# Key and value compression in one set of float32r products instead of two sets of fp32 products

## The chip, the cores and the metric

The kernel runs on 1 core of one Trainium2 chip. The metric is device microseconds of one execution; three runs of the kernel before gave a median of 1655.65 us (1655.62 to 1655.7).

## The reference, cut to what matters

One decoder layer for 512 tokens of width 2048. A wide input projection feeds a sparse attention (mixer A) and a gated MLP (mixer B). The part that is changed is the first step of the attention's compressed branch: for keys and for values, blocks of 32 tokens at a stride of 16 are flattened together with a position embedding and go through a small two-layer network.

```python
def compress(kv, pe, w1, w2):
    b, s, g, d = kv.shape
    ch = kv.reshape(b, s // CMP_STRIDE, CMP_STRIDE, g, d)
    nc = s // CMP_STRIDE - CMP_RATIO + 1
    blocks = jnp.concatenate([ch[:, r:nc + r] for r in range(CMP_RATIO)], axis=2)
    blocks = blocks + pe[None, None, :, None, :]
    hid = jax.nn.silu(jnp.einsum('bnlgd,lde->bnge', blocks, w1))
    return jnp.einsum('bnge,ef->bngf', hid, w2)

kc = compress(k_c, pe_k, w1_k, w2_k)
vc = compress(v_c, pe_v, w1_v, w2_v)
```

There are 4 groups of 64 channels, so a block is 32 x 64 = 2048 numbers, and w1 is 2048 x 64 for keys and again for values.

## The kernel before, in words

**The stream of projections.** All large products are jobs of one generator, `gemm` (L170). A job is one block of columns of a weight matrix. Of kind "T" it holds 128 output columns, with the 512 tokens as the moving operand; each of its 16 steps over the 2048 inputs is one unit of three TensorE products (L190 to L192): the weights' high float32r part by the activations' high and low parts, and the weights' low part by the high part. Kind "N" has the tokens as the stationary operand (L198 to L200). A float32r part is a rounded copy (the high part) or what that rounding left (the low part). The weights are split while they stream in: SyncE's queue loads `raw`, ScalarE casts the high part (`high`, L98), VectorE subtracts for the low part (`low`, L104). `split_to` (L143) does this two sub-blocks of four steps ahead for the low part and three ahead for the high part. A job's evacuation `evac` empties its PSUM bank at the end; parts of it can be put off in `deferred`, which `flush` runs. `background` is a queue of small pieces of ScalarE and VectorE work, of which each sub-block takes two (`state["pops"]`).

**The order.** The program text fixes the order on each engine. `fill(n)` (L228) issues n more units of the stream, `finish(name)` (L232) issues units until that job is done. Everything that is not a projection is placed between such calls by hand. The jobs around the change are, in order, kc0, kc1 (compressed keys), vc0, vc1 (compressed values), k00, k01, k10, k11 (other keys), vs, vw (other values), q0, z0 and so on.

**The compression.** `evac_c` (L314) copies each of the four banks into `tokk` or `tokv`, fp32 tiles with two tokens folded onto the 128 partitions (64 channels each): two ScalarE copies (L320, L321) and two VectorE copies (L324, L325). Two further columns per tile hold the position embedding, put there after vc0 by a transpose (L680) and copies (L682, L683). After vc1, `hidden` (L687) runs once for keys and once for values: 16 fp32 products of 128 x 64 weights by 132 columns (4 groups of 32 blocks and one more), into one bank, with `fill(1)` after every fourth; then VectorE adds the embedding's part (L696, L698), ScalarE takes a tanh (L700), VectorE finishes SiLU (L701 to L708). The second layer is L717 (keys) and L722 (values), after which the stream goes on to q1. Between these stand `fill(4)`, `fill(6)` and `fill(6)`, so that with the eight inside `hidden` 24 units of k00 and k01 lie between the end of vc1 and L717.

**Other names the prediction uses.** `evac_k` (L249) empties the banks of k00 to k11 with four ScalarE casts (L254) and four VectorE subtractions (L256). `evac_v` (L260) empties those of vs and vw; L266 is a tanh on a part of vw's bank. `bank` (L68) hands out a whole PSUM bank, two to each of four tags. `o32` (L645) is a 16 KB per partition tile that the gates and the attention's outputs use later on.

Of the kernel before, what the change touches and what calls it, by code (L numbers as in the profile page):

```python
# [12 lines left out]
F32 = mybir.dt.float32  # L13
F32R = mybir.dt.float32r
BF16 = mybir.dt.bfloat16
AF = mybir.ActivationFunctionType
ALU = mybir.AluOpType
# [3 lines left out]
P = 128  # L21
# [3 lines left out]
KT = D // P  # L25
HEADS = 16
GROUPS = 4
HD = 64
NCMP = 32
EPS = 1e-6  # L30
MASKED = -3.0e32
C_Q, C_KV, C_G, C_ZA, C_UV, C_ZB, C_M = 0, 1024, 2560, 2608, 3632, 5680, 6704
# [19 lines left out]
def kernel(ctx: ExitStack, tc: tile.TileContext, x, p, norm_g, w_in,  # L52
                      pe_k, w1_k, w2_k, pe_v, w1_v, w2_v, ln_g, ln_b, sgu_w, sgu_b,
                      w_up_a, w_up_b, w_out, w_ple, w_ple_gate, final_g, out):
    nc = tc.nc
    x, out = x[0], out[0]
    p = p[0, 0]
    norm_g, w_in, ln_g, ln_b, sgu_w, sgu_b = norm_g[0], w_in[0], ln_g[0], ln_b[0], sgu_w[0], sgu_b[0]
    pe_k, w1_k, w2_k, pe_v, w1_v, w2_v = pe_k[0], w1_k[0], w2_k[0], pe_v[0], w1_v[0], w2_v[0]
# [8 lines left out]
    def bank(kind, name):  # L68
        return psum.tile([P, 512], F32, tag=kind, name=name)
# [26 lines left out]
    def high(hi, src, scale=None):  # L96
        if scale is None:
            nc.scalar.copy(hi, src)  # L98
        else:
            nc.scalar.mul(hi, src, scale)  # L100

    def low(hi, lo, src, scale=None):
        if scale is None:
            nc.vector.tensor_tensor(out=lo, in0=src, in1=hi.bitcast(F32), op=ALU.subtract)  # L104
        else:
            nc.vector.scalar_tensor_tensor(out=lo, in0=src, scalar=scale, in1=hi.bitcast(F32),
                                           op0=ALU.mult, op1=ALU.subtract)

    def split(hi, lo, src, scale=None, later=False):

        high(hi, src, scale)
        if later:
            deferred.append(lambda: low(hi, lo, src, scale))
        else:
            low(hi, lo, src, scale)
# [3 lines left out]
    background = deque()  # L119

    def add_job(job):
        first = 0
        while first < job.kt:
            n = min(job.per_load, job.kt - first)
            loads.append((job, first, n))
            for k in range(first, first + n, job.per_sub):
                subs.append((job, k, min(job.per_sub, first + n - k), len(loads) - 1))
            first += n
        jobs.append(job)
# [98 lines left out]
    def fill(n):  # L228
        for _ in range(n):
            next(run, None)  # L230

    def finish(name):  # L232
        while name not in done:
            next(run)
        flush()
# [76 lines left out]
    tok = {}  # L312

    def evac_c(which, a):  # L314
        def f(ps):
            t = tok[which]
            g0, g1 = 2 * a, 2 * a + 1
            src = ps.rearrange("p (n o e) -> p e o n", n=NCMP, o=8)
            lo_r, up_r = slice(0, 64), slice(64, 128)
            nc.scalar.copy(t[lo_r, :, g0, :NCMP], src[lo_r, 0])  # L320
            nc.scalar.copy(t[up_r, :, g0, :NCMP], src[lo_r, 1])  # L321

            def rest():
                nc.vector.tensor_copy(t[up_r, :, g1, :NCMP], src[up_r, 1])  # L324
                nc.vector.tensor_copy(t[lo_r, :, g1, :NCMP], src[up_r, 0])  # L325
            deferred.append(rest)
        return f

# [18 lines left out]
        add_job(Job(f"pl{cg}", "N", w_ple, 512 * cg, 512, 2, lambda k: (pl_in["h"][:, k], pl_in["l"][:, k]),  # L347
                    evac_ple(cg), (xs, ys)[cg % 2]))
    for a in range(2):
        add_job(Job(f"kc{a}", "T", w_in, C_KV + 128 * a, 128, KT, h_act, evac_c("k", a)))  # L350
    for a in range(2):
        add_job(Job(f"vc{a}", "T", w_in, C_KV + 256 + 128 * a, 128, KT, h_act, evac_c("v", a)))
    for b, c in ((0, 512), (1, 1024)):
        for a in range(2):
            add_job(Job(f"k{b}{a}", "T", w_in, C_KV + c + 128 * a, 128, KT, h_act, evac_k(b, a)))
# [190 lines left out]
    with tc.tile_pool(name="xin", bufs=4, side="right") as xin:  # L546
# [7 lines left out]
        st = xin.tile([P, TT, 2], F32, name="st", bufs=1)  # L554
# [35 lines left out]
        for j in range(2):  # L590
            b = bank("t", "ps_p")
# [4 lines left out]
        b = bank("o", "ps_g")  # L596
# [46 lines left out]
    vc = mid.tile([P, GROUPS, HD], F32, name="vc")  # L643
    orow = ph_o.enter_context(tc.tile_pool(name="orow", bufs=1, side="right"))
    o32 = orow.tile([P, 8, S], F32, name="o32")  # L645
# [14 lines left out]
                            base=-31, channel_multiplier=1)  # L660

    with tc.tile_pool(name="cmp", bufs=1) as cmp:
        w1t, w2t, pet = {}, {}, {}
        for n in "kv":
            tok[n] = cmp.tile([P, 8, GROUPS, NCMP + 2], F32, name="tok" + n)
            nc.gpsimd.memset(tok[n][:, :, :, NCMP:], 0.0)
        for n, w1, w2, pe in (("k", w1_k, w2_k, pe_k), ("v", w1_v, w2_v, pe_v)):
            w1t[n] = cmp.tile([P, 16, HD], F32, name="w1" + n)
            w2t[n] = cmp.tile([HD, 2, HD], F32, name="w2" + n)
            pet[n] = cmp.tile([NCMP, 2, HD], F32, name="pe" + n)  # L670
            for i in range(2):
                nc.gpsimd.dma_start(pet[n][:, i], pe)
        for n, w1, w2 in (("k", w1_k, w2_k), ("v", w1_v, w2_v)):
            nc.gpsimd.dma_start(w1t[n], w1.rearrange("l d e -> (l d) e").rearrange("(m p) e -> p m e", p=P))
            for i in range(2):
                nc.gpsimd.dma_start(w2t[n][:, i], w2)
        finish("vc0")
        for n in "kv":
            b = bank("t", "ps_pe")
            nc.tensor.transpose(b[:, :NCMP], pet[n].rearrange("l i d -> l (i d)"), ident[:NCMP, :NCMP])  # L680
            src = b[:, :NCMP].rearrange("p (s o e) -> p e o s", s=2, o=8)
            nc.vector.tensor_copy(tok[n][0:64, :, 0, NCMP:], src[0:64, 0])  # L682
            nc.vector.tensor_copy(tok[n][64:128, :, 0, NCMP:], src[64:128, 1])  # L683
        finish("vc1")
        hid = {}

        def hidden(n):  # L687
            b = bank("o", "ps_hid")
            o = b[:HD, :132].rearrange("p (g n) -> p g n", g=GROUPS)
            for m in range(16):  # L690
                nc.tensor.matmul(o, w1t[n][:, m], tok[n][:, m % 8, :, m // 8:m // 8 + NCMP + 1],
                                 start=m == 0, stop=m == 15)
                if m % 4 == 3:
                    fill(1)
            c = cmp.tile([HD, 1], F32, name="c" + n)
            nc.vector.tensor_copy(c, b[:HD, 32:33])  # L696
            y = cmp.tile([HD, GROUPS, NCMP], F32, name="y" + n)
            nc.vector.tensor_scalar(out=y, in0=o[:, :, :NCMP], scalar1=c, scalar2=None, op0=ALU.add)  # L698
            t = cmp.tile([HD, GROUPS, NCMP], F32, name="t" + n)
            nc.scalar.activation(t, y, AF.Tanh, scale=0.5)  # L700
            nc.vector.scalar_tensor_tensor(out=y, in0=t, scalar=1.0, in1=y, op0=ALU.add, op1=ALU.mult)  # L701
            if n == "k":
                h = cmp.tile([HD, GROUPS, NCMP], F32, name="hidk")
                nc.vector.tensor_scalar(out=h, in0=y, scalar1=0.5, scalar2=None, op0=ALU.mult)
            else:
                h = cmp.tile([HD, GROUPS, 4, NCMP], F32, name="hidv")
                for r in range(4):
                    nc.vector.tensor_scalar(out=h[:, :, r], in0=y, scalar1=0.5, scalar2=None, op0=ALU.mult)  # L708
            hid[n] = h

        fill(4)
        hidden("k")
        fill(6)
        hidden("v")
        fill(6)
        b = bank("o", "ps_kc")
        nc.tensor.matmul(b[:, :128], w2t["k"].rearrange("e i f -> e (i f)"),  # L717
                         hid["k"].rearrange("e g n -> e (g n)"), start=True, stop=True)
        split(kc_h, kc_l, b[:, :128].rearrange("p (g n) -> p g n", g=GROUPS))
        b = bank("o", "ps_vc")  # L720
        for g in range(GROUPS):
            nc.tensor.matmul(b[:, g * HD:g * HD + HD], hid["v"][:, g].rearrange("e r n -> e (r n)"),  # L722
                             w2t["v"][:, 0], start=True, stop=True)
        nc.vector.tensor_copy(vc, b[:, :256].rearrange("p (g d) -> p g d", g=GROUPS))
        finish("q1")

# [190 lines left out]
    n = len(slots)  # L917
# [40 lines left out]
    with tc.tile_pool(name="mlp", bufs=1) as mlp:  # L958
        vn = mlp.tile([P, TT, 1024], F32, name="vn")
        st = mlp.tile([P, TT, 2, 6], F32, name="bst")  # L960
# [10 lines left out]
        for hf in range(2):  # L971
            b = bank("o", "ps_w")
            for j in range(4):
                nc.tensor.transpose(b[:, j * P:j * P + P], ws[:, 4 * hf + j], ident)
            nc.vector.tensor_tensor(out=ws[:, 4 * hf:4 * hf + 4], in0=b.rearrange("p (g t) -> p g t", g=4),
                                    in1=tri.unsqueeze(1).to_broadcast([P, 4, P]), op=ALU.mult)
# [3 lines left out]
        with tc.tile_pool(name="uzp", bufs=1) as uzp:  # L980
# [36 lines left out]
            for g in range(8):  # L1017
# [3 lines left out]
                for gg in ((0, 1, 2) if g == 2 else (g,)):  # L1021
                    b = bank("st"[gg % 2], "ps_sv")
                    for c in range(TT):
                        nc.tensor.matmul(b[:, c * P:c * P + P], vn[:, c, gg * P:gg * P + P], ws[:, gg],
                                         start=True, stop=True)
                    sv = vn[:, :, gg * P:gg * P + P]
                    nc.vector.tensor_tensor(out=sv, in0=b.rearrange("p (c t) -> p c t", c=TT),
                                            in1=bs[:, gg].unsqueeze(1).to_broadcast([P, TT, P]), op=ALU.add)
                    nc.gpsimd.tensor_tensor(out=uz[:, gg].rearrange("p (c t) -> p c t", c=TT),
                                            in0=uz[:, gg].rearrange("p (c t) -> p c t", c=TT), in1=sv, op=ALU.mult)  # L1030
# [17 lines left out]
    for cg in range(4):  # L1048
# [50 lines left out]
```

## Time and profile before

| | |
|---|---|
| median of three runs | 1655.65 us |
| the profiled execution, its own time | 1655.33 us |
| its span, first to last instruction | 1653.6 us |
| TensorE (PE) busy in the span | 1639.1 us |
| VectorE (DVE) busy | 742.8 us |
| ScalarE (ACT) busy | 612.9 us |
| GpSimd (POOL) busy | 114.0 us |
| the two runs of `hidden`, first to last product's start | 84.1 to 102.7 us of the span |

How to read it: a row of the timeline gives the start in us from the span's start, the duration, the engine (PEld is TensorE's weight load), the line, the operation, the tile written and those read, the shapes and a count of merged instructions; in brackets stands the idle time of the engine ahead of it and what ended it. A matmul's shown duration is longer than the step from one start to the next, since they are pipelined, so costs are taken from the steps between starts. An fp32 product shows as two records (the 16 products of one `hidden` are x32). The times are of one execution; its own time is 1.7 us above its span.

### The profile page before, as it was taken

How to read it: one execution, taken by the hardware profiler on the slowest of the kernel's cores; microseconds unless marked ns; L12 is line 12 of the kernel's file. 1: busy time of each engine (PE TensorE's matmuls, PEld its weight loads, DVE VectorE, ACT ScalarE, POOL GpSimd, SP SyncE). 2: the span in 40 equal slices, each digit the busy share in tenths (PEclk: the TensorE clock that was granted, in tenths of full speed). 3: DMA queues.
4: the chain of work that ended last, by engine and by line, in shares of the span. 5: the costliest groups of instructions: out<-in, count | busy, mean ns of one | idle time of the engine just before them, and what ended most of it. 6: DMA issues, size and time to landing. Idle time of an engine off the chain costs nothing.

```text
span 1653.6 us, 20567 instructions
## 1 busy us (share of the span) xinstructions
PE 1639.1 (99%) x7837; PEld 1367.1 (83%) x7837; DVE 742.8 (45%) x1486; ACT 612.9 (37%) x1229; POOL 114.0 (7%) x145
## 2 busy tenths in 40 slices
PE   9999999999999999999999999999999999999997
PEld 7879988888888888888888888888888888888886
DVE  6443368888874363344222232223223433333335
ACT  7333356666663332233222222222223322223335
POOL 1200000110110001000000000000000000000001
PEclk9999999999999999999999999999999999999999
DMA  8522421111115333333333333333333533363333
GB/s 318 130 60 81 113 64 52 52 45 46 51 52 153 95 96 89 90 96 95 102 90 102 97 95 102 90 101 96 95 101 91 203 90 90 99 218 92 100 101 128
DMA packets 217186, 168.02 MB, mean 102 GB/s; under 512 B 4976, under 2 KB 190976, under 8 KB 215552
## 3 DMA queue, kind: packets, MB, share of 16 engines
q1 hardware_dynamic: 213472, 151.57, 32.7%
q0 software_dynamic: 3472, 14.79, 2.5%
q8 instruction: 61, 1.00, 0.2%
q14 instruction: 37, 0.30, 0.1%
q10 hardware_dynamic: 144, 0.36, 0.1%
HBM read 158.31 MB, written 8.39 MB: 101 GB/s over the span
## 4 chain that ended last, share of the span: by engine, by line
PE 97%; DVE 2%; ACT 1%; DMA 0%; issue 0%; DVEq 0%; SPq 0%; ACTq 0%
PE ps_wo L198 4%; PE ps_wo L200 4%; PE ps_mb L191 4%; PE ps_ma L191 4%; PE ps_ma L190 4%; PE ps_mb L192 4%; PE ps_mb L190 4%; PE ps_ma L192 4%; PE ps_wo L199 4%; PE ps_pg L198 3%; PE ps_pg L199 3%; PE ps_pg L200 3%; PE ps_t L805 2%; PE ps_za L190 2%; PE ps_za L192 2%; PE ps_za L191 2%
## 5 line engine op out<-in xcount | busy, mean ns | idle before, releaser
L104 DVE TENSOR_TENSOR lo<-raw,hi 128x512 fp32r<-128x512 f32 (+1 forms) x536 | 366.7, 687 | 641.0 <-PE ps_mb L192 129.5
L98 ACT CAST hi<-raw 128x512 fp32r<-128x512 f32 (+1 forms) x536 | 328.2, 615 | 724.1 <-PE ps_wo L200 99.2
L198 PE MATMUL ps_wo<-hi,act_h 128*128 128x512 f32 x256 | 101.0, 395 | 0.1
L200 PE MATMUL ps_wo<-hi,act_l 128*128 128x512 f32 x256 | 99.8, 390 | 0.0
L199 PE MATMUL ps_wo<-lo,act_h 128*128 128x512 f32 x256 | 99.7, 390 | 0.0
L190 PE MATMUL ps_ma<-act_h,hi 128*128 128x512 f32 x256 | 99.6, 389 | 0.0
L191 PE MATMUL ps_ma<-act_l,hi 128*128 128x512 f32 x256 | 99.6, 389 | 0.0
L192 PE MATMUL ps_ma<-act_h,lo 128*128 128x512 f32 x256 | 99.6, 389 | 0.0
L190 PE MATMUL ps_mb<-act_h,hi 128*128 128x512 f32 x256 | 99.6, 389 | 0.0
L191 PE MATMUL ps_mb<-act_l,hi 128*128 128x512 f32 x256 | 99.6, 389 | 0.0
L192 PE MATMUL ps_mb<-act_h,lo 128*128 128x512 f32 x256 | 99.6, 389 | 0.0
L98 ACT CAST pth<-ps_t 128x512 fp32r<-128x512 f32 (+1 forms) x88 | 48.0, 546 | 65.6 <-PE ps_t L805 65.3
L766 ACT ACTIVATE prob<-prob,st 128x512 f32<-128x512 f32 (+3 forms) x128 | 70.6, 555 | 3.9 <-DVE st L757 3.7
L444 POOL TENSOR_TENSOR m<-sig,sig 128x512 f32<-128x512 f32 x16 | 27.0, 1690 | 582.3 <-DVE sig L442 464.1
L104 DVE TENSOR_TENSOR ptl<-ps_t,pth 128x512 fp32r<-128x512 f32 (+1 forms) x88 | 56.2, 638 | 21.5 <-ACT pth L98 20.6
L757 DVE CUSTOM_DVE_ANT_0 prob<-ps_s,b 128x512 f32<-128x512 f32 (+3 forms) x128 | 56.3, 486 | 9.8 <-PE ps_s L754 9.4
L200 PEld LDWEIGHTS ps_wo<-hi,act_l 128*128 128x128 f32 x256 | 48.1, 188 | 10.3
L198 PEld LDWEIGHTS ps_wo<-hi,act_h 128*128 128x128 f32 x256 | 48.1, 188 | 10.1 <-DVE sig L442 0.5
L190 PEld LDWEIGHTS ps_mb<-act_h,hi 128*128 128x128 f32 x256 | 48.1, 188 | 10.0
L190 PEld LDWEIGHTS ps_ma<-act_h,hi 128*128 128x128 f32 x256 | 48.1, 188 | 10.0
L192 PEld LDWEIGHTS ps_ma<-act_h,lo 128*128 128x128 f32 x256 | 48.1, 188 | 10.0
L191 PEld LDWEIGHTS ps_mb<-act_l,hi 128*128 128x128 f32 x256 | 48.1, 188 | 9.9
(317 smaller groups left out, 3672.2 us busy)
## 6 DMA issues: line engine op xcount, KB each, us to landing
raw<-in_w_in_dram SPq DMA_DIRECT2D x164, 512.0 KB, 3.7
raw<-in_w_out_dram SPq DMA_DIRECT2D x32, 512.0 KB, 3.6
raw<-in_w_ple_gate_dram SPq DMA_DIRECT2D x32, 512.0 KB, 3.6
raw<-in_w_up_a_dram SPq DMA_DIRECT2D x16, 512.0 KB, 3.8
raw<-in_w_up_b_dram SPq DMA_DIRECT2D x16, 512.0 KB, 3.8
xt<-in_x_dram SPq DMA_DIRECT2D x4, 1024.0 KB, 11.5
spill<-ple POOLq DMA_DIRECT2D x4, 1024.0 KB, 6.8
m<-in_x_dram POOLq DMA_DIRECT2D x4, 1024.0 KB, 7.3
```

What stands on the lines that cost most here:

```text
L98: nc.scalar.copy(hi, src)
L104: nc.vector.tensor_tensor(out=lo, in0=src, in1=hi.bitcast(F32), op=ALU.subtract)
L190: nc.tensor.matmul(ps, hi[:, j], ah, start=st, stop=False)
L191: nc.tensor.matmul(ps, hi[:, j], al, start=False, stop=False)
L192: nc.tensor.matmul(ps, lo[:, j], ah, start=False, stop=sp)
L198: nc.tensor.matmul(o, ah[:, sl], hi[:, j], start=st, stop=False)
L199: nc.tensor.matmul(o, ah[:, sl], lo[:, j], start=False, stop=False)
L200: nc.tensor.matmul(o, al[:, sl], hi[:, j], start=False, stop=sp)
L444: nc.gpsimd.tensor_tensor(out=merge_tiles["m"][:, f], in0=merge_tiles[0], in1=t, op=ALU.add)
L757: nc.vector.tensor_tensor_reduce(out=pt[:, j * n:j * n + n], in0=o[:, j], in1=b0[:, 512 - n:], scale=-SLOPE[h], scalar=3.0e38, op0=ALU.add ...
L766: nc.scalar.activation(sl, sl, AF.Exp, bias=st[:, 0, j, hh:hh + 1], scale=-1.0, accum_out=st[:, 1, j, hh:hh + 1])
L805: nc.tensor.transpose(b[:, (2 * e + hh) * P:(2 * e + hh + 1) * P], pts[hh][:, c:c + P], ident)
```

## The change

Keys and values go through the first layer together, in float32r parts:

- The token tiles become `tokh` and `tokl`, a high and a low float32r part of 128 x 8 x 2 x 4 x 34, with keys and values side by side. `evac_c` now makes four ScalarE copies (high) and, put off in `deferred`, four VectorE subtractions (low) for each bank. The embedding's copies get a low part too.
- The two w1 matrices are loaded by the same GpSimd queue into `o32`, and are split into `w1h` and `w1l`, with keys' and values' 64 columns side by side, by four pieces of `background` that vc1's first two sub-blocks take up.
- The first layer is one loop of 16 steps with three products each: weights 128 x 128 by 272 columns (2 x 4 x 34). The first eight steps go to one bank, the last eight to another. Of the 128 x 272 results only keys by keys and values by values are used. ScalarE copies the first bank to `o32` after step 8; VectorE adds the shifted halves and the embedding's part, for the two halves of the partitions apart; then tanh and SiLU run once for both.
- Units of the stream around it: `fill(3)`, four inside the loop, `fill(8)`: 15 instead of 24 ahead of the second layer, which itself keeps its products.

```diff
     def evac_c(which, a):
         def f(ps):
-            t = tok[which]
-            g0, g1 = 2 * a, 2 * a + 1
+            th, tl = (tok[i][:, :, which] for i in "hl")
             src = ps.rearrange("p (n o e) -> p e o n", n=NCMP, o=8)
-            lo_r, up_r = slice(0, 64), slice(64, 128)
-            nc.scalar.copy(t[lo_r, :, g0, :NCMP], src[lo_r, 0])
-            nc.scalar.copy(t[up_r, :, g0, :NCMP], src[lo_r, 1])
+            halves = slice(0, 64), slice(64, 128)
+            part = [(halves[e], halves[r], 2 * a + r, e) for r in range(2) for e in range(2)]
+            for dst, srow, g, e in part:
+                nc.scalar.copy(th[dst, :, g, :NCMP], src[srow, e])
 
             def rest():
-                nc.vector.tensor_copy(t[up_r, :, g1, :NCMP], src[up_r, 1])
-                nc.vector.tensor_copy(t[lo_r, :, g1, :NCMP], src[up_r, 0])
+                for dst, srow, g, e in part:
+                    nc.vector.tensor_tensor(out=tl[dst, :, g, :NCMP], in0=src[srow, e],
+                                            in1=th[dst, :, g, :NCMP].bitcast(F32), op=ALU.subtract)
             deferred.append(rest)
...
+            for e, rows in enumerate((slice(0, 64), slice(64, 128))):
+                h, l = (tok[i][rows, :, n, 0, NCMP:] for i in "hl")
+                nc.vector.tensor_copy(h, src[rows, e])
+                nc.vector.tensor_tensor(out=l, in0=src[rows, e], in1=h.bitcast(F32), op=ALU.subtract)
+            for c in (slice(0, 8), slice(8, 16)):
+                background.append(lambda n=n, c=c: split(w1t["h"][:, c, n], w1t["l"][:, c, n], w1r[n][:, c]))
         finish("vc1")
...
+        while background:
+            fill(1)
+        fill(3)
+        hid = [bank("o", f"ps_hid{i}")[:, :8 * (NCMP + 2)] for i in range(2)]
+        for m in range(16):
+            o, st, sp = hid[m // 8], m % 8 == 0, m % 8 == 7
+            th, tl = (tok[i][:, m % 8].rearrange("p s g n -> p (s g n)") for i in "hl")
+            wh, wl = (w1t[i][:, m].rearrange("p s e -> p (s e)") for i in "hl")
+            nc.tensor.matmul(o, wh, th, start=st, stop=False)
+            nc.tensor.matmul(o, wh, tl, start=False, stop=False)
+            nc.tensor.matmul(o, wl, th, start=False, stop=sp)
+            if m == 7:
+                nc.scalar.copy(o32[:, 6, :8 * (NCMP + 2)], o)
+            if m % 4 == 3:
+                fill(1)
...
+        for n, rows in enumerate((lo_r, up_r)):
+            o, q = (t[rows].rearrange("p (s g n) -> p s g n", s=2, g=GROUPS)[:, n]
+                    for t in (o32[:, 6, :8 * (NCMP + 2)], hid[1]))
+            nc.vector.tensor_tensor(out=c[rows], in0=o[:, 0, NCMP:NCMP + 1], in1=q[:, 0, NCMP + 1:], op=ALU.add)
+            nc.vector.scalar_tensor_tensor(out=y[rows], in0=o[:, :, :NCMP], scalar=c[rows], in1=q[:, :, 1:NCMP + 1],
+                                           op0=ALU.add, op1=ALU.add)
+        nc.scalar.activation(t, y, AF.Tanh, scale=0.5)
+        nc.vector.scalar_tensor_tensor(out=y, in0=t, scalar=1.0, in1=y, op0=ALU.add, op1=ALU.mult)
+        for r in range(4):
+            nc.vector.tensor_scalar(out=h[:, :, r], in0=y, scalar1=0.5, scalar2=None, op0=ALU.mult)
+        fill(8)
```

More of the change, by code (lines that the diff above doesn't have):

```diff
@@ L349 @@
     for a in range(2):
-        add_job(Job(f"kc{a}", "T", w_in, C_KV + 128 * a, 128, KT, h_act, evac_c("k", a)))
+        add_job(Job(f"kc{a}", "T", w_in, C_KV + 128 * a, 128, KT, h_act, evac_c(0, a)))
     for a in range(2):
-        add_job(Job(f"vc{a}", "T", w_in, C_KV + 256 + 128 * a, 128, KT, h_act, evac_c("v", a)))
+        add_job(Job(f"vc{a}", "T", w_in, C_KV + 256 + 128 * a, 128, KT, h_act, evac_c(1, a)))
     for b, c in ((0, 512), (1, 1024)):
@@ L662 @@
     with tc.tile_pool(name="cmp", bufs=1) as cmp:
[L663 to L670, printed above, removed]
+        w1t, pet = {}, {}
+        for i in "hl":
+            tok[i] = cmp.tile([P, 8, 2, GROUPS, NCMP + 2], F32R, name="tok" + i)
+            nc.gpsimd.memset(tok[i].bitcast(F32)[:, :, :, :, NCMP:], 0.0)
+            w1t[i] = cmp.tile([P, 16, 2, HD], F32R, name="w1" + i)
+        w2t = o32[:, 4, 256:384].rearrange("p (i e) -> p i e", i=2)
+        for n, pe in enumerate((pe_k, pe_v)):
+            pet[n] = cmp.tile([NCMP, 2, HD], F32, name=f"pe{n}")
             for i in range(2):
                 nc.gpsimd.dma_start(pet[n][:, i], pe)
-        for n, w1, w2 in (("k", w1_k, w2_k), ("v", w1_v, w2_v)):
-            nc.gpsimd.dma_start(w1t[n], w1.rearrange("l d e -> (l d) e").rearrange("(m p) e -> p m e", p=P))
+        w1r = [o32[:, 2 * n:2 * n + 2].rearrange("p a (m e) -> p (a m) e", e=HD) for n in range(2)]
+        for n, w1 in enumerate((w1_k, w1_v)):
+            nc.gpsimd.dma_start(w1r[n], w1.rearrange("l d e -> (l d) e").rearrange("(m p) e -> p m e", p=P))
+        for n, w2 in enumerate((w2_k, w2_v)):
             for i in range(2):
-                nc.gpsimd.dma_start(w2t[n][:, i], w2)
+                nc.gpsimd.dma_start(w2t[64 * n:64 * n + 64, i], w2)
         finish("vc0")
-        for n in "kv":
+        for n in range(2):
             b = bank("t", "ps_pe")
@@ L681 @@
             src = b[:, :NCMP].rearrange("p (s o e) -> p e o s", s=2, o=8)
-            nc.vector.tensor_copy(tok[n][0:64, :, 0, NCMP:], src[0:64, 0])
-            nc.vector.tensor_copy(tok[n][64:128, :, 0, NCMP:], src[64:128, 1])
-        finish("vc1")
[L685 to L715, printed above, removed]
+            for e, rows in enumerate((slice(0, 64), slice(64, 128))):
[4 more added lines that the diff above has]
+                background.append(lambda n=n, c=c: split(w1t["h"][:, c, n], w1t["l"][:, c, n], w1r[n][:, c]))
@@ new lines @@
+        y = o32[:, 4, 0:128].rearrange("p (g n) -> p g n", g=GROUPS)
+        t = o32[:, 4, 128:256].rearrange("p (g n) -> p g n", g=GROUPS)
+        h = o32[:, 5].rearrange("p (g r n) -> p g r n", g=GROUPS, r=4)
+        c = cmp.tile([P, 1], F32, name="hid_c")
+        lo_r, up_r = slice(0, 64), slice(64, 128)
+        for n, rows in enumerate((lo_r, up_r)):
[4 more added lines that the diff above has]
+                                           op0=ALU.add, op1=ALU.add)
@@ L716 @@
+        nc.scalar.activation(t, y, AF.Tanh, scale=0.5)
[3 more added lines that the diff above has]
+        fill(8)
         b = bank("o", "ps_kc")
-        nc.tensor.matmul(b[:, :128], w2t["k"].rearrange("e i f -> e (i f)"),
-                         hid["k"].rearrange("e g n -> e (g n)"), start=True, stop=True)
+        nc.tensor.matmul(b[:, :128], w2t[lo_r].rearrange("e i f -> e (i f)"), h[lo_r, :, 0], start=True, stop=True)
@@ L721 @@
         for g in range(GROUPS):
-            nc.tensor.matmul(b[:, g * HD:g * HD + HD], hid["v"][:, g].rearrange("e r n -> e (r n)"),
-                             w2t["v"][:, 0], start=True, stop=True)
+            nc.tensor.matmul(b[:, g * HD:g * HD + HD], h[up_r, g].rearrange("e r n -> e (r n)"), w2t[up_r, 0],
+                             start=True, stop=True)
         nc.vector.tensor_copy(vc, b[:, :256].rearrange("p (g d) -> p g d", g=GROUPS))
```

## Prediction

> **What bounds the kernel now.** I read the profile's page first: busy times, slices, and the chain that ended last.
>
> ```profile
> PE 1639.1 (99%) x7837; PEld 1367.1 (83%) x7837; DVE 742.8 (45%) x1486; ACT 612.9 (37%) x1229; POOL 114.0 (7%) x145
> PEclk9999999999999999999999999999999999999999
> PE 97%; DVE 2%; ACT 1%; DMA 0%; issue 0%; DVEq 0%; SPq 0%; ACTq 0%
> ```
>
> TensorE is busy nearly throughout, at full granted clock, and makes 97% of the chain. So a microsecond taken off TensorE's queue comes off the end, and a wait put into it is added; work on the other engines counts only where TensorE waits for it. The change sits at 70 to 110 us of the span, so next comes TensorE's timeline there.
>
> ```profile
> 81.34 0.39 PE L190 MATMUL ps_k<-act_h,hi 128*128 128x512 f32 x1
> 83.83 0.39 PE L192 MATMUL ps_k<-act_h,lo 128*128 128x512 f32 x1
> 84.15 1.11 PE L691 MATMUL ps_hid<-tokk,w1k 128*64 128x132 f32 x8
> 85.19 0.50 PE L190 MATMUL ps_k<-act_h,hi 128*128 128x512 f32 x1
> 86.08 1.11 PE L691 MATMUL ps_hid<-tokk,w1k 128*64 128x132 f32 x8
> 89.97 1.11 PE L691 MATMUL ps_hid<-tokk,w1k 128*64 128x132 f32 x8
> ```
>
> From 81.34 to 83.83 are 11 steps of the stream: 2.49 / 11 = 0.227 us a product, 0.68 us a unit. From the first to the last of the four blocks of fp32 products are three periods, (89.97 - 84.15) / 3 = 1.94 us, each one block and one unit. **A block costs 1.94 - 0.68 = 1.26 us**, its turns into and out of fp32 included. The eight blocks cost 8 x 1.26 = 10.1 us.
>
> **The change part by part.** *The new products.* The trace has no float32r product of 272 columns, but it has them with 128 x 128 weights at 256 and 304.
>
> ```profile
> 149.97 0.28 PE L198 MATMUL ps_vs<-hi,act_h 128*128 128x256 f32 x1
> 153.93 0.28 PE L198 MATMUL ps_vs<-hi,act_h 128*128 128x256 f32 x1
> 160.77 0.30 PE L198 MATMUL ps_vw<-hi,act_h 128*128 128x304 f32 x1
> 167.39 0.30 PE L198 MATMUL ps_vw<-hi,act_h 128*128 128x304 f32 x1
> ```
>
> At 256 columns there are 33 products between the two rows, 3.96 / 33 = 0.120 us each; at 304 there are 48, 6.62 / 48 = 0.138 us. The price at 272 lies between; a third of the way gives 0.126. **16 x 3 = 48 products cost 6.05 us** (5.8 to 6.6). They follow float32r products, so I count no turn. This gains 10.1 - 6.05 = 4.05 us.
>
> *The first wait.* The second product of the new loop reads `tokl`, which is complete only when vc1's bank has been through four ScalarE copies and four VectorE subtractions. These rows show how it is emptied now:
>
> ```profile
> 81.54 0.37 ACT L320 COPY tokv<-ps_vc 64x256 f32<-64x256 f32 x1 [2.28 <-PE ps_vc L192]
> 81.92 0.36 ACT L321 COPY tokv<-ps_vc 64x256 f32<-64x256 f32 x1
> 82.31 0.43 DVE L324 COPY tokv<-ps_vc 64x256 f32<-64x256 f32 x1 [2.75 <-ACT tokv L321]
> 82.75 0.43 DVE L325 COPY tokv<-ps_vc 64x256 f32<-64x256 f32 x1
> 126.22 2.36 ACT L254 CAST ob_h<-ps_k 64x512 fp32r<-64x512 f32 x4 [2.29 <-PE ps_k L192]
> 128.61 2.80 DVE L256 TENSOR_TENSOR ob_l<-ps_k,ob_h 64x512 fp32r<-64x512 f32 x4 [4.37 <-ACT ob_h L254]
> 186.70 0.42 DVE L104 TENSOR_TENSOR vt<-ps_vw,vt 128x256 fp32r<-128x256 f32 x1 [0.32 <-ACT vt L98]
> 187.16 0.21 ACT L266 ACTIVATE gates<-ps_vw 128x48 f32<-128x48 f32 x1 [0.49 <-DVE vt L104]
> ```
>
> L324 needs nothing that L320 or L321 produce, and still starts 0.03 us after L321's end. In `evac_k` the first of four subtractions needs the first cast alone, and starts when all four have ended (126.22 + 2.36). L266 reads other columns than the subtraction it waits for. So two engines on one PSUM tile go one after the other, in program order. The four copies start at 81.54, 0.38 apart, and end at 81.54 + 3 x 0.38 + 0.37 = 83.05; the subtractions, taken at the 0.44 step and 0.43 duration of the 64x256 copies (a 64x512 one takes 2.80 / 4 = 0.70, half of it 0.35), run from 83.09 to 83.09 + 3 x 0.44 + 0.43 = 84.84. TensorE answers 0.05 us later, as at 132.19 below: 84.89. With `fill(3)` it gets there at 81.34 + 9 x 0.227 = 83.38 with the first product, which needs only `tokh`, and at 83.51 with the second. It stands for 84.89 - 83.51 = 1.38 us. Before, `fill(4)` and a ready tile by 83.18 hid this.
>
> *What a stand costs beyond itself, and a second wait.* The same kind of wait exists after evacuations by `evac_k`:
>
> ```profile
> 120.11 1.90 DVE L104 TENSOR_TENSOR lo<-raw,hi 128x512 fp32r<-128x512 f32 x3
> 120.12 0.39 PE L190 MATMUL ps_k<-act_h,hi 128*128 128x512 f32 x1
> 120.35 0.39 PE L191 MATMUL ps_k<-act_l,hi 128*128 128x512 f32 x1
> 120.86 0.50 PE L192 MATMUL ps_k<-act_h,lo 128*128 128x512 f32 x1
> 121.20 0.40 PE L190 MATMUL ps_k<-act_h,hi 128*128 128x512 f32 x1
> 123.98 0.39 PE L190 MATMUL ps_k<-act_h,hi 128*128 128x512 f32 x1
> 132.19 0.19 PEld L192 LDWEIGHTS ps_k<-act_h,lo 128*128 128x128 f32 x1 [0.54 <-DVE lo L104]
> ...
> PEld ps_k L192 <- DVE lo L104: 1.1, 2, 0.5
> ```
>
> VectorE comes late with `lo` because it was held by L256. From 120.12 to 123.98 are 15 steps, 15 x 0.227 = 3.40 in steady flow, 3.86 here: 0.46 us lost. The stand itself is 120.86 - 120.35 - 0.227 = 0.28; the restart takes the other 0.18. Hence the first wait costs **1.38 + 0.18 = 1.56 us**. The last row, from the list of waits (us in total, times, longest), counts it twice: after k01 and after k10. After k00 it is absent, since the values' fp32 blocks slowed TensorE there. In the new order L722 stands one unit ahead of k00's end (3 + 4 + 8 = 15 of 16), nothing slows k01, and VectorE and ScalarE meet the same queue: **0.46 us** for a third such wait, zero at the least.
>
> *VectorE's and ScalarE's added work.* In vc1 VectorE gets two more instructions for vc0's bank, four more small ones for the embedding, and four splits of 128x512, all queued around the stream's own.
>
> ```profile
> 70.19 0.37 ACT L320 COPY tokv<-ps_vc 64x256 f32<-64x256 f32 x1 [2.28 <-PE ps_vc L192]
> 71.85 0.17 DVE L682 COPY tokk<-ps_pe 64x16 f32<-64x16 f32 x1
> 72.03 0.18 DVE L683 COPY tokk<-ps_pe 64x16 f32<-64x16 f32 x1
> 72.61 1.51 DVE L104 TENSOR_TENSOR lo<-raw,hi 128x512 fp32r<-128x512 f32 x2
> 76.35 0.39 PE L192 MATMUL ps_vc<-act_h,lo 128*128 128x512 f32 x1
> ...
> L104 DVE TENSOR_TENSOR lo<-raw,hi 128x512 fp32r<-128x512 f32 (+1 forms) x536 | 366.7, 687 | 641.0 <-PE ps_mb L192 129.5
> ...
> 54.65 1.06 POOL L676 DMA_DIRECT2D w2v<-in_cmp_w_v_dram  x2
> DMA to landing us min/median/max: 7.6/7.6/7.6
> ```
>
> The first `lo`, now at 72.61, then follows copies to 71.70, four subtractions to 73.5 and eight small ones of 0.2, to 75.1; it ends at 75.8, and the product that needs it is the one at 76.35. The margin is 0.5 us, so I count nothing. Then two splits and a `lo` by turns, 0.69 each, end at 79.9, ahead of their products (79.1 for the next, done at 77.8; 81.8 for the one after). ScalarE's share, a cast ahead of each, ends sooner. The w1 loads keep GpSimd's queue, whose last issues of this group are over at 54.65 + 1.06; with w1v's 7.6 us to landing (last row) the data are there at 64, covered by 7 us and more. If any cover goes, the price is what it is late by.
>
> *Behind the loop.* ScalarE's copy of the first bank waits for step 8 in ScalarE's queue, ahead of casts not due for two sub-blocks. The loop ends at 84.89 + 46 x 0.126 + 4 x 0.68, about 93.5. VectorE's chain goes by these rows:
>
> ```profile
> 106.11 0.34 DVE L698 TENSOR_SCALAR yv<-ps_hid,cv 64x128 f32<-64x128 f32 x1
> 106.49 0.31 ACT L700 ACTIVATE tv<-yv 64x128 f32<-64x128 f32 x1 [3.63 <-DVE yv L698]
> 107.15 0.63 DVE L708 TENSOR_SCALAR hidv<-yv 64x128 f32<-64x128 f32 x4
> ```
>
> Four additions and a product at yv's 0.34, the tanh at 0.31, the halving at 0.63 and some gaps make about 3 us; `fill(8)` covers 8 x 0.68 = 5.4. It costs nothing. The second layer keeps its products and its price.
>
> **The sum:** 4.05 - 1.56 - 0.46 = 2.0 us gained. The span goes to 1651.6, the profiled execution to 1653.3, and the median, which stands 0.3 us above it, from 1655.65 to **1653.6 us**. That is 0.12%, inside the 0.2% (3.3 us) that a measurement of this kernel can tell from no change.
>
> **Rivals.** *A shorter first wait.* If a bank is shared by partitions, the first two subtractions, which read the lower 64 rows, start after the second copy at 82.31, and the third and fourth after the last, at 83.2: `tokl` is ready at 84.06, TensorE stands 0.6 us and loses 0.78, and the time is 1652.85. Taken to its end (only the last subtraction behind the last copy) it costs nothing: with no k00 wait either, the gain is 4.05, **1651.6**. Against it: L324 reads the upper rows while L320 and L321 read the lower, and waits. The Trainium skill, "PSUM — Partial Sum Buffer", section Terms, says that engines are kept apart per bank and 32-partition quadrant, and that different quadrants of a bank may be used at the same time. The trace does not agree that this kernel profits from it: L324's 0.03 us behind L321 is a whole-bank order.
>
> *No wait after k00.* Then 0.46 comes back: 1653.15. For it: the casts ahead may stand differently; against: k01 and k10 lose the same.
>
> *VectorE late in vc1.* If the small instructions or the w1 splits run longer than counted, the 0.5 us margin goes and one more restart comes on top: up to 1 us, 1654.6.
>
> *Slower than before: 272 columns don't go at the pace of 256 and 304.* The loop stands or falls with its 48 prices. It breaks even at (10.1 - 2.0) / 48 = 0.168 us a product, and is 0.2% slower from 0.24. At the fp32 pace, 1.04 us for four products of 132 columns (0.0020 us a column), a product would take 0.54: 25.7 us, and 1673. For it: weights of 128 columns change at every second product. Against it: so they do at 256 columns, at 0.120.
>
> *The change doesn't do what it says:* were the products fp32 after all, this same 1673.
>
> **How the numbers follow.** Forecast with both waits: 0.62. Shorter first wait 0.15, half of that beyond 0.2% faster; no k00 wait alone 0.08; VectorE late 0.09; slower pace or fp32 0.06. So faster by over 0.2% is 0.08, slower 0.06, the rest 0.86 within. The range takes the product's bounds (5.8 to 6.6 us), no wait at all at the low end, and a late VectorE at the high end: 4.05 + 0.25 = 4.3 gained, and 10.1 - 6.6 - 2.0 - 1.0 = 0.5 gained: 1651.4 to 1655.1.
>
> **What would show it.** Right: 48 products 0.12 to 0.13 us apart; a stand of about 1.4 us at the loop's second product, ended by VectorE's subtraction into `tokl`; that subtraction's first start just behind ScalarE's fourth copy; stands of 0.5 us by weight loads of k-jobs three times, not two. Wrong: the subtractions start among the copies, the loop's steps are above 0.14, or TensorE waits in vc1 for `lo` or at the second layer.

## The result, and the profile after

| | before | after |
|---|---|---|
| median of 22 runs each | 1655.66 us | 1653.18 us (1652.87 to 1653.61) |
| the profiled execution, its span | 1653.6 us | 1651.4 us |
| first product of k00 to first product of vs | 81.34 to 137.35: 56.01 us | 81.55 to 135.14: 53.59 us |
| from there to the end of the span | 1516.25 us | 1516.26 us |

The ratio is 0.9985, 95% interval 0.9979 to 0.9992: 2.5 us or 0.15% faster, a small change, but the interval does not reach 1. The table's last two rows place it: all of it, 2.42 us, is won between k00 and vs, and nothing follows from it later. (That the after execution reached k00 0.2 us later comes from its start and varies from run to run; the stretch from k00 to vs doesn't contain it, and I compare runs by it.)

The page of the kernel after, busy time by engine:

```profile
PE 1635.9 (99%) x7821; PEld 1366.8 (83%) x7821; DVE 749.5 (45%) x1500; ACT 617.5 (37%) x1241; POOL 114.5 (7%) x145
```

The first product of vs, with which the stretch ends, before and then after:

```profile
137.35 0.28 PE L198 MATMUL ps_vs<-hi,act_h 128*128 128x256 f32 x1
```

```profile
135.14 0.28 PE L198 MATMUL ps_vs<-hi,act_h 128*128 128x256 f32 x1
```

TensorE is as full as before. VectorE has 6.7 us more to do and ScalarE 4.6; this is the price of splitting, and it lies beside TensorE's work. Now TensorE's timeline at k00's first product, the new loop, its step, the second layer, and the product that waits after k00:

```profile
81.55 0.39 PE L190 MATMUL ps_k<-act_h,hi 128*128 128x512 f32 x1
...
83.60 0.29 PE L700 MATMUL ps_hid<-tokh,w1h 128*128 128x272 f32 x1
85.16 0.36 PE L701 MATMUL ps_hid<-tokl,w1h 128*128 128x272 f32 x1 [1.28 <-DVE tokl L325]
85.36 0.29 PE L702 MATMUL ps_hid<-tokh,w1l 128*128 128x272 f32 x1
...
87.31 0.29 PE L700 MATMUL ps_hid<-tokh,w1h 128*128 128x272 f32 x1
...
88.69 0.29 PE L702 MATMUL ps_hid<-tokh,w1l 128*128 128x272 f32 x1
...
99.10 0.39 PE L192 MATMUL ps_k<-act_h,lo 128*128 128x512 f32 x1
99.42 0.37 PE L724 MATMUL ps_kc<-o 64*128 64x128 f32 x1
99.42 0.43 PE L728 MATMUL ps_vc<-o 64*128 64x64 f32 x2
...
101.02 0.40 PE L192 MATMUL ps_k<-act_h,lo 128*128 128x512 f32 x1
...
106.71 0.39 PE L190 MATMUL ps_k<-act_h,hi 128*128 128x512 f32 x1
106.94 0.39 PE L191 MATMUL ps_k<-act_l,hi 128*128 128x512 f32 x1
107.43 0.50 PE L192 MATMUL ps_k<-act_h,lo 128*128 128x512 f32 x1
...
110.50 0.39 PE L190 MATMUL ps_k<-act_h,hi 128*128 128x512 f32 x1
```

From 87.31 to 88.69 are 11 steps of 0.1255 us. The second product starts 1.56 us after the first where 0.125 would do: a stand of 1.43, and the bracket names VectorE's subtraction into `tokl`. From 106.71 to 110.50 are 15 steps, 3.79 us where 3.40 would do: the wait after k00, 0.39. ScalarE and VectorE at vc1's bank:

```profile
81.75 1.51 ACT L321 CAST tokh<-ps_vc 64x256 fp32r<-64x256 f32 x4 [2.28 <-PE ps_vc L192]
```

```profile
83.29 1.73 DVE L325 TENSOR_TENSOR tokl<-ps_vc,tokh 64x256 fp32r<-64x256 f32 x4 [2.98 <-ACT tokh L321]
```

VectorE begins 0.03 us behind the fourth copy's end (81.75 + 1.51) and ends at 85.02, 0.14 us ahead of TensorE's second product. The list of TensorE's waits for weights (us in total, times, longest) has the third wait for `lo`:

```profile
PEld ps_k L192 <- DVE lo L104: 1.6, 3, 0.5
```

### The profile page after: what moved, and what is told of

Read it like the earlier page. It is cut to its first block, busy times and chain, and to the rows that moved or that the text cites. A ratio compares the mean times of both kernels' runs of the same rounds, so it can differ in the third digit from the quotient of the medians.

```text
span 1651.4 us, 20568 instructions
## 1 busy us (share of the span) xinstructions
PE 1635.9 (99%) x7821; PEld 1366.8 (83%) x7821; DVE 749.5 (45%) x1500; ACT 617.5 (37%) x1241; POOL 114.5 (7%) x145
## 4 chain that ended last, share of the span: by engine, by line
PE 92%; DVE 2%; ACT 1%; issue 0%; DVEq 0%; ACTq 0%
PE ps_wo L198 4%; PE ps_ma L190 4%; PE ps_mb L190 4%; PE ps_mb L192 4%; PE ps_mb L191 4%; PE ps_ma L192 4%; PE ps_ma L191 4%; PE ps_wo L200 4%; PE ps_wo L199 4%; PE ps_pg L198 3%; PE ps_pg L199 3%; PE ps_pg L200 3%; PE ps_t L811 2%; PE ps_za L190 2%; PE ps_za L192 2%; PE ps_za L191 2%
## 5 line engine op out<-in xcount | busy, mean ns | idle before, releaser
L198 PEld LDWEIGHTS ps_wo<-hi,act_h 128*128 128x128 f32 x256 | 48.1, 188 | 10.1 <-DVE sig L443 0.5
L192 PEld LDWEIGHTS ps_mb<-act_h,lo 128*128 128x128 f32 x256 | 48.0, 188 | 10.0
L191 PEld LDWEIGHTS ps_ma<-act_l,hi 128*128 128x128 f32 x256 | 48.0, 188 | 10.0
```

What stands on the lines that cost most here:

```text
L191: nc.tensor.matmul(ps, hi[:, j], al, start=False, stop=False)
L192: nc.tensor.matmul(ps, lo[:, j], ah, start=False, stop=sp)
L198: nc.tensor.matmul(o, ah[:, sl], hi[:, j], start=st, stop=False)
```

## The experiments

Times are medians in device us; "stretch" is k00's first product to vs's first, 53.59 us in the changed kernel. From vs to the end every kernel took 1516.2 to 1516.5 us. e6 is an edit of the kernel before, all others are edits of the changed kernel. Where one execution stands, its time is that of the profiled one.

| run | median us | ratio to before, 95% | stretch us |
|---|---|---|---|
| e1_fill5 | 1651.92 | 0.9977 (0.9968 to 0.9986) | 52.27 |
| e2_fill12 | 1652.84 | 0.9983 (0.9974 to 0.9991) | 53.23 |
| e3_fill16 | 1651.37 | 0.9973 (0.9963 to 0.9984) | 51.65 |
| e4_fill16_14 | 1650.96 | 0.9972 (0.9962 to 0.9983) | 51.25 |
| e5_pairs | 1653.10, one execution | | 53.68 |
| e6_before_rows | 1655.24, one execution | | 55.70 |
| e7_fill1 | 1656.31, one execution | | 56.53 |
| e8_apart | 1651.60, one execution | | 52.42 |
| e9_values_first | 1653.61 | 0.9988 (0.9979 to 0.9998) | 53.92 |
| e10_three | 1651.13 | 0.9973 (0.9963 to 0.9984) | 51.18 |
| e11_fill2 | 1655.60, one execution | | 55.85 |
| e12_apart_again | 1651.91 | 0.9977 (0.9968 to 0.9986) | 52.41 |

**e1_fill5: cover the first wait.**

```diff
-        fill(3)
+        fill(5)
...
-        fill(8)
+        fill(6)
```

> Five units instead of three ahead of the loop, six instead of eight behind it; the same work. Theory (the first wait is TensorE getting to the second product before VectorE has finished the low part of vc1's bank): two units more are 0.91 us of cover per... 2 x 0.68 = 1.36 us in all, against a stand of 1.43, so the stand at the second product falls to under 0.1 us and the time falls by 1.4 to 1.55 us from the changed kernel, to about 1651.7. Rival (the stand is a cost of starting products with other weights or of TensorE's queue, and not of VectorE): the stand stays, within 0.2 us of 1653.2.

TensorE at the loop's start in e1_fill5:

```profile
85.14 0.29 PE L700 MATMUL ps_hid<-tokh,w1h 128*128 128x272 f32 x1
85.35 0.36 PE L701 MATMUL ps_hid<-tokl,w1h 128*128 128x272 f32 x1
85.55 0.29 PE L702 MATMUL ps_hid<-tokh,w1l 128*128 128x272 f32 x1
```

The step to the second product is 0.21 instead of 1.56 us, and the stretch 1.32 shorter, a little less than the 1.4 to 1.55 that I expected. The stand was VectorE's lateness; two units cover nearly all of it, and 0.16 us remain in the first two steps. VectorE still sets the second product's start: it comes 3.62 us after k00's first product, against 3.61 in the changed kernel.

**e2_fill12: cover the wait after k00.** `fill(8)` becomes `fill(12)`.

> Twelve units instead of eight behind the loop, so that the second layer stands in k01 and not ahead of k00's end; the same work. Theory (after k00 TensorE overtakes VectorE, which is held by the subtractions of k00's bank): the second layer's 1.2 us now lie between that evacuation and the product that waited, so the wait of 0.26 us with its restart, 0.39 in all, goes: about 1652.8, and two waits for lo by k-jobs are left in place of three. Rival (the wait is due to VectorE's chain behind the loop): three waits stay, 1653.2.

The stretch is 0.36 us shorter, and one wait for `lo` is gone from the list of waits for weights:

```profile
PEld ps_k L192 <- DVE lo L104: 1.1, 2, 0.5
```

The second layer, put behind k00's evacuation, takes the place of the stand there. The rival is out.

**e3_fill16 and e4_fill16_14: both, and one more.** e3 has `fill(16)` ahead of the loop, e4 has `fill(14)` behind it too.

> Sixteen units ahead of the loop, so that the loop runs in k01, behind k00's end. Theory: both waits go, the first because the low part has been ready for long, that after k00 because the loop holds TensorE back: 1.55 + 0.39 us less than the changed kernel, about 1651.2, 0.27% under the kernel before. Rival (VectorE, held by k00's bank, now comes late at the second layer, whose chain is eight units long): a stand of up to 1 us at the second layer, 1652.

> Sixteen units ahead of the loop and fourteen behind it, so that the loop stands in k01 and the second layer in k10, each behind an evacuation of a k-job. Theory: as the kernel with sixteen units, and the wait after k01 (0.4 to 0.46 us) goes too, one wait for lo by k-jobs is left: about 1650.8. Rival: the second layer stands too far ahead of the product that waits, or moves the wait to another place: no better than sixteen units alone, 1651.2.

e3's stretch is 1.94 us under the changed kernel's, as 1.55 + 0.39 said. e4 takes 0.40 more, and its list has one wait for `lo` left, `0.5, 1, 0.5`. **e4 is the fastest kernel of the study by its median, 4.7 us or 0.28% under the kernel before**; the changed kernel had a little over half of this.

**e5_pairs: do rows of a bank come free apart?**

```diff
-            for dst, srow, g, e in part:
-                nc.scalar.copy(th[dst, :, g, :NCMP], src[srow, e])
...
+            for r in range(2):
+                for dst, srow, g, e in part[2 * r:2 * r + 2]:
+                    nc.scalar.copy(th[dst, :, g, :NCMP], src[srow, e])
+                for dst, srow, g, e in part[2 * r:2 * r + 2]:
+                    nc.vector.tensor_tensor(out=tl[dst, :, g, :NCMP], in0=src[srow, e],
+                                            in1=th[dst, :, g, :NCMP].bitcast(F32), op=ALU.subtract)
```

The subtractions are issued at once and no longer put off in `deferred`.

> The bank's evacuation in another program order: two copies (lower rows), their two subtractions, two copies (upper rows), their two subtractions, for each of the four banks; the same work. Theory (two engines on one bank take turns in program order, whatever the rows): the third copy starts only behind the second subtraction, VectorE ends with vc1's bank 0.05 to 0.1 us later than in the changed kernel, and the stand at the second product stays at 1.4 to 1.5 us. Rival (rows of a bank are free apart): the upper rows' copies run beside the lower rows' subtractions, VectorE ends 0.75 us earlier and the stand falls to 0.7.

ScalarE, VectorE and TensorE at vc1's bank in e5_pairs:

```profile
83.22 0.75 ACT L322 CAST tokh<-ps_vc 64x256 fp32r<-64x256 f32 x2 [0.91 <-DVE tokl L324]
```

```profile
82.34 0.85 DVE L324 TENSOR_TENSOR tokl<-ps_vc,tokh 64x256 fp32r<-64x256 f32 x2 [2.19 <-ACT tokh L322]
84.00 0.87 DVE L324 TENSOR_TENSOR tokl<-ps_vc,tokh 64x256 fp32r<-64x256 f32 x2 [0.82 <-ACT tokh L322]
```

```profile
84.11 0.36 PE L698 MATMUL ps_hid<-tokh,w1h 128*128 128x272 f32 x1 [0.55 <-ACT tokh L322]
85.02 0.36 PE L699 MATMUL ps_hid<-tokl,w1h 128*128 128x272 f32 x1 [0.54 <-DVE tokl L324]
```

ScalarE's copies of rows 64 to 127 wait until VectorE is through with rows 0 to 63 (82.34 + 0.85 = 83.19). The bank is handed over whole, VectorE ends no sooner (3.51 us after k00's first product, against 3.47), and the stretch is 0.09 us longer. The second product's own stand is shorter than the theory said, 0.91 - 0.125 = 0.79 us and so near the rival's 0.7, but only because the first product now waits 0.7 us for the upper rows of `tokh`; together they stand as long as before. What orders the two engines is not the tile `tokh` or `tokl` as a whole: in e8 TensorE reads the keys' columns of `tokl` from 83.36 on while VectorE writes the values' columns until 84.74. Here the kernel as it runs differs from what the Trainium skill, "PSUM — Partial Sum Buffer", Terms, allows, namely two engines on different quadrants of one bank; whether the chip would bear it no run here shows, as the waits are in the program.

**e6_before_rows: the second layer on two halves of the rows.** The second layer had become 0.22 us cheaper, which I had not forecast. In the kernel before, the values' hidden units and w2 go to partitions 64 to 127:

```diff
-                h = cmp.tile([HD, GROUPS, 4, NCMP], F32, name="hidv")
+                h = cmp.tile([P, GROUPS, 4, NCMP], F32, name="hidv")[64:128]
...
-                             w2t["v"][:, 0], start=True, stop=True)
+                             w2t["v"][64:128, 0], start=True, stop=True)
```

> The kernel before, with the values' second layer (its weights and its hidden units) on partitions 64 to 127 instead of 0 to 63; all else as it was. Theory (in the changed kernel the second layer lost 1.24 us instead of 1.46 because the keys' and the values' products lie on different halves of the rows and run side by side): the loss falls to about 1.24 here too, and the first values' product starts with the first keys' product. Rival (it is due to what runs ahead of it, float32r products instead of fp32 ones, or to the other operand's shape): it stays at 1.46.

TensorE in e6_before_rows:

```profile
107.76 0.39 PE L192 MATMUL ps_k<-act_h,lo 128*128 128x512 f32 x1
108.08 0.37 PE L717 MATMUL ps_kc<-hidk,w2k 64*128 64x128 f32 x1
108.10 0.42 PE L722 MATMUL ps_vc<-w2v,hidv 64*128 64x64 f32 x2
...
109.68 0.40 PE L192 MATMUL ps_k<-act_h,lo 128*128 128x512 f32 x1
```

The same place in the kernel before:

```profile
107.54 0.39 PE L192 MATMUL ps_k<-act_h,lo 128*128 128x512 f32 x1
...
109.68 0.40 PE L192 MATMUL ps_k<-act_h,lo 128*128 128x512 f32 x1
```

From 107.76 to 109.68 are 1.92 us with three steps of 0.227 in them: 1.24 lost, as in the changed kernel (99.10 to 101.02), against 1.46 before (107.54 to 109.68). The first values' product starts 0.02 us after the first keys' product. The rows alone did it. The Trainium skill, "TensorEngine Tiling (Array Packing)", Key Properties, says that different tiles of the array can work in parallel and that each is tied to its partitions; the trace agrees.

**e7_fill1 and e11_fill2: the wait made larger.** One and two units ahead of the loop, ten and nine behind it.

> One unit instead of three ahead of the loop, ten instead of eight behind it; the same work. Theory (VectorE's end sets when the second product starts, whatever TensorE does before): the stand grows by the two units' 1.36 us, less what the first product itself waits for the high part, to about 2.8 us in all, and the time to about 1654.6; the second product starts within 0.1 us of where it did. Rival (a fixed cost at the loop's start): the stand stays 1.4 us.

> The changed kernel with two units instead of three ahead of the loop and nine instead of eight behind it. Theory A (the clock falls to half only when the stands together pass some bound between 1.4 and 2.4 us, and 0.3 + 1.4 us are below it): the stand grows by one unit's 0.68 us, the granted clock stays at 1.00, 1653.9. Theory B (two stands are enough): the products step at 0.227 us for about 3.3 us, 1655.5.

Both were slower than my expectation for a pure stand: 2.94 and 2.26 us in the stretch where 1.36 and 0.68 were due. e7's loop start, and its granted clock in the window from 85.60 to 89.00 (0.51, the number ahead of the DMA share):

```profile
83.61 0.36 PE L700 MATMUL ps_hid<-tokh,w1h 128*128 128x272 f32 x1 [1.01 <-ACT tokh L321]
85.37 0.36 PE L701 MATMUL ps_hid<-tokl,w1h 128*128 128x272 f32 x1 [1.40 <-DVE tokl L325]
85.57 0.33 PE L702 MATMUL ps_hid<-tokh,w1l 128*128 128x272 f32 x1
85.69 0.43 PE L700 MATMUL ps_hid<-tokh,w1h 128*128 128x272 f32 x1
85.92 0.43 PE L701 MATMUL ps_hid<-tokl,w1h 128*128 128x272 f32 x1
```

```profile
85.60:89.00 3.40, 3.40 (x14) 3.12 (x14) 0.35 (x1) 0.00 (x0) 0.00 (x0) 0.51 0.00 0
```

The second product starts where it did, 3.61 us after k00's first product, so VectorE sets it, as the theory has it. But then the products step at 0.23 us where 0.1255 would do, at half the granted clock, for 3.4 us. That loses 45% of the time, about 1.55 us: 1.36 + 1.55 = 2.91 against 2.94. In e11 the stands are 0.33 and 1.40 us, and the clock still falls:

```profile
83.60 0.36 PE L700 MATMUL ps_hid<-tokh,w1h 128*128 128x272 f32 x1 [0.33 <-ACT tokh L321]
85.36 0.43 PE L701 MATMUL ps_hid<-tokl,w1h 128*128 128x272 f32 x1 [1.40 <-DVE tokl L325]
```

```profile
86.00:87.00 1.00, 1.00 (x7) 1.00 (x6) 0.00 (x0) 0.00 (x0) 0.00 (x0) 0.50 0.00 0
```

Theory B has the time right (1655.60), and A's bound is wrong. But two stands alone are not enough: e5 has two, 0.55 and 0.54 us with a product between them, and kept 1.00, like the changed kernel with one bracketed idle time of 1.28 us.

The traces also record when the granted clock rises and falls. In all fourteen the time from the clock's rise, 4 to 7 us into the span, to its next fall is a whole multiple of 3.413 us: 23 times that in e7 and e11, 480 to 482 times, at the kernel's end, in the others. I call the points at such distances marks. Between two marks e7 has 2.41 us of idle time and e11 1.73, and the clock falls at the second mark. The most without a fall is 1.28 us, in e2, whose stand lies whole between two marks; in the changed kernel a mark cuts the stand into 0.21 and 1.07 us. So a bound on the idle time between marks, somewhere from 1.28 to 1.73 us, fits every run. A bound on the longest single stand, 1.40 us in e7 and e11, fits too, and no run tells the two apart.

The Trainium skill, "TensorE: Matmul & The Clock Gate", Part 1, has a free-running activity window of about 3.4 us; the length of the slow stretch, 3.41 us, agrees with it. Its table asks for an idle window; here 1.73 us of idleness with a product between them was enough.

**e8_apart, e12_apart_again and e9_values_first: is it the joining that pays?** Keys and values in 96 smaller float32r products, keys first; e9 has the values first.

```diff
-        for m in range(16):
-            o, st, sp = hid[m // 8], m % 8 == 0, m % 8 == 7
-            th, tl = (tok[i][:, m % 8].rearrange("p s g n -> p (s g n)") for i in "hl")
-            wh, wl = (w1t[i][:, m].rearrange("p s e -> p (s e)") for i in "hl")
+        for s in range(2):
+            for m in range(16):
+                o, st, sp = hid[m // 8][0:HD, half * s:half * s + half], m % 8 == 0, m % 8 == 7
+                th, tl = (tok[i][:, m % 8, s].rearrange("p g n -> p (g n)") for i in "hl")
+                wh, wl = (w1t[i][:, m, s] for i in "hl")
```

> Keys and values apart, still as three float32r products: 96 products of 128 x 64 weights by 136 columns in place of 48 of 128 x 128 by 272, with the units of the stream around them as in the changed kernel. Theory (a product has a floor near the 0.12 us seen at 256 columns): 96 x 0.12 = 11.5 us, 5.5 us slower than the changed kernel, about 1658.7, slower than the kernel before. Rival (the step goes with the columns): 0.064 us a product, 6.1 us, as the changed kernel, 1653.2.

> The run with keys and values apart, keys first, timed. Theory: 96 products at 0.064 us make 6.1 us, no stand, three waits for lo by k-jobs: 1.55 us under the changed kernel, 1651.6.

> Keys and values apart, in 96 products, as in the run that was 1.5 us faster than the changed kernel, but with the values' half first. Theory (that run gained nothing by its products, 6.1 us against 6.0, and all by beginning with keys, whose low part is ready since kc1): with values first the stand of about 1.4 us at the second product is back, and the time is that of the changed kernel, 1653.0 to 1653.3. Rival (smaller products are what gained): no stand, 1651.6.

My first expectation was wrong by 7 us. TensorE in e8_apart:

```profile
83.36 0.23 PE L703 MATMUL ps_hid<-tokl,w1h 128*64 128x136 f32 x1
...
84.77 0.23 PE L704 MATMUL ps_hid<-tokh,w1l 128*64 128x136 f32 x1
84.83 0.44 PE L190 MATMUL ps_k<-act_h,hi 128*128 128x512 f32 x1
85.11 0.39 PE L191 MATMUL ps_k<-act_l,hi 128*128 128x512 f32 x1
```

From 83.36 to 84.77 are 22 steps of 0.064 us: half of 0.1255 for half the columns, with weights half as wide. 96 x 0.064 = 6.1 us against 48 x 0.1255 = 6.0. There is no floor near 0.12 here. And the second product (83.36) doesn't stand, since it reads the keys' part of `tokl`, ready since kc1. So the time falls by 1.27 us (e12, which times this kernel again), not by the 1.55 expected. e9 tells the smaller products and the order apart; its second product:

```profile
85.39 0.25 PE L703 MATMUL ps_hid<-tokl,w1h 128*64 128x136 f32 x1 [1.35 <-DVE tokl L325]
```

With the values first the stand is back, and the stretch is 1.51 us over e12's. The small products gain nothing; beginning with what is ready does. They even cost a little: e9 has the changed kernel's stand and its three waits for `lo`, and its stretch is 53.92 - 53.59 = 0.33 us longer, which is about what e12 lacks of the 1.55.

**e10_three: each piece behind a k-job.** e8 with `fill(16)` ahead of the keys' loop, `fill(14)` ahead of the values' and `fill(14)` behind it.

> Keys and values apart, and each piece behind an evacuation of a k-job: the keys' loop at the start of k01, the values' loop at the start of k10, the second layer at the start of k11. Theory: no stand in the loops, and none of the three waits for lo by k-jobs behind k00, k01 and k10 (0.4 to 0.46 us each): 1650.4 to 1650.7, 0.4 us under the kernel with sixteen and fourteen units. Rival (what is taken from these waits comes back at a later job): not under 1650.9.

No wait for `lo` by a k-job is in its list, but the stretch is only 0.07 us under e4's, and the median, 1651.13, misses what I expected and lies where the rival put it. In the stretch the rival's reason is not seen: what the third wait gave back goes to the smaller products. The first projection after each of four blocks steps 0.28 us and not 0.227 (84.83 to 85.11 above), 4 x 0.05 = 0.2, and the products take 0.1 more, together the 0.33 that e9 shows. Behind the stretch this execution takes 0.2 us more than e4's (1516.48 against 1516.29), lost in one step ahead of products into `ps_c` at 439 us of the span; whether the new order causes that is open.

## Why the prediction was right

The forecast was 2.0 us, the measured gain 2.5, inside the 0.2% that was forecast as no change; the places were those named. As the limit of what can be told from no change, 0.2% was too wide: the interval, 0.9979 to 0.9992, does not reach 1.

- **The fp32 blocks and the new products.** 48 at 0.126 was forecast, 0.1255 measured: 6.02 us. The rival of a slower pace is out.
- **The first wait.** Forecast 1.56 us with its restart. Measured: 1.43 of stand, 0.08 in the next step, 0.04 in slightly slower steps around the loop, 1.55 in all. VectorE ended where forecast, at 85.02 - 0.21 = 84.81 on the old clock against 84.84, but TensorE answered 0.14 us later and not 0.05, and the restart cost 0.12 and not 0.18: that the sum agrees to 0.01 us is luck. VectorE ran whole-bank behind ScalarE (e5), and with the wait covered its price came back, 1.32 of it in e1 and all in e3.
- **The wait after k00.** Forecast 0.46, measured 0.39; its place and cause are shown by e2.
- **Work in vc1.** The first `lo` was to end at 75.8, with a margin of 0.5 us. VectorE's row in the kernel after, whose stream is 0.2 us later:

```profile
75.39 0.69 DVE L104 TENSOR_TENSOR lo<-raw,hi 128x512 fp32r<-128x512 f32 x1
```

It ended at 76.08 - 0.21 = 75.87 on the old clock, and TensorE did not wait.

- **Behind the loop.** "The second layer keeps its products and its price" is the step that failed: products the same, price 0.22 us less, since the values moved to the upper rows (e6). With it the sum is 10.1 - 6.02 - 1.55 - 0.39 + 0.22 = 2.36 against 2.42 in the stretch.

What the prediction left unsaid is that joining keys and values is what makes the first wait: the loop's second product needs the values' last subtraction, while the kernel before began with keys (e12, e9). Its sentence on the kernel before, that `fill(4)` and a tile ready by 83.18 hid the wait, names the wrong tile: 83.18 is the end of the copies into `tokv`, which the first run of `hidden` does not read. It reads `tokk`, complete since 72.2, and `tokv` is first read at 96.0.

## What to carry to other kernels

When an fp32 product on the path is replaced by split products, price the split where the last input arrives, not only the products: here 4.1 us were won on TensorE and 1.55 lost to an evacuation that had become twice as long and lay directly ahead. Place such a block behind work that needs none of its inputs, best where another wait stands anyway (e3, e4), and start it with the part that is ready first. Joining two products into one larger one saved 0.33 us here (e9) and made both halves wait for the later one, which cost 1.55; measure the pace of the smaller products before you accept such a wait.

## What the runs showed of the hardware

- A float32r product of 128 x 64 weights by 136 columns steps at 0.064 us, one of 128 x 128 by 272 at 0.1255: proportional, with no floor at 0.12 us.
- Stands of 0.33 and 1.40 us with one product between them halved TensorE's granted clock for 3.4 us (e11), about 1.6 us lost; a single idle time of 1.28 us did not, nor did two of 0.55 and 0.54 (e5). The clock changed only at marks 3.413 us apart, so where a stand falls between them may count as well as its length. The changed kernel was one unit of the stream, 0.68 us, away from that. The two executions with a fall don't tell where the bound lies, or whether it is one on the idle time between marks or on the longest stand.
- fp32 products on partitions 0 to 63 and 64 to 127 ran side by side and took 0.22 us off a block of ten records.
